# Attention's maxima through a diagonal block on the core instead of a row through DRAM, with another order of the work that fills its gaps

## Chip, core and metric

One core of a Trainium2 chip runs the whole program. The metric is the device time of one execution in microseconds (us). Engines: PE is TensorE (matrix products), DVE is VectorE, ACT is ScalarE, POOL is GpSimd, SP is the engine whose queue issues the transfers (DMA).

## What is computed

The reference is a backbone of two layers over 512 latent and 256 context tokens of width 1024: attention with a gated convolutional network behind it, then a state-space mixer with another such network. The change lies in the attention of the first layer: 16 query heads of 64 over 4 key heads, 768 tokens in all.

```python
s = jnp.einsum('bqhgd,bkhd->bhgqk', q, k).astype(jnp.float32) * (HEAD_DIM ** -0.5)
p = jax.nn.softmax(s, axis=-1).astype(v.dtype)
return jnp.einsum('bhgqk,bkhd->bqhgd', p, v)
```

Latent queries see all 768 keys, context queries the 256 context keys. The softmax needs each query's largest score, or some value near it, to be taken off before the exponential. Query and key gains are eight times the usual here, so the scores are large.

## The kernel before, in words

Heads are worked on in 8 pairs. The two heads of a pair lie on partitions 0 to 63 and 64 to 127, so each product of a pair comes as two of 64 rows that run beside each other. Tensors of the exact path are split into a high and a low part and multiplied three times.

**Maxima of a pair** (`Pair.maxima`, L588 to L617). For each tile of 128 queries the score with the high parts alone (`ps_m`, L593) goes to PSUM with queries on partitions, and a reduction on DVE (L595) takes the negated largest value per query: over the latent keys into `lat` (`ma`), over the context keys into `ctx` (`mb`). A minimum on DVE (L612) joins them into `mx`; context queries take a copy (L615). Since the scores proper have keys on partitions and queries along the free dimension, the maxima must become a row. `row` (L598 to L603) writes them to DRAM as single elements (`mrow_d<-mx`, L602) and reads them back as a row on partition 0 or 64 of `mrow` (L603), for each head, first for the four latent tiles and then for the two context tiles. All transfers are issued by SP in order.

**Scores, exponential and values of a pair** (`Pair.steps`). Seven steps: six tiles of 128 keys against the 512 latent queries, and one for the context queries. In each step six score products (L664, three for each head) and then two products of a row of ones with `mrow` (L667) add up in `ps_s`: the last ones add the negated maximum of the query to every key. ACT takes the exponential (L668, `pr`), DVE adds it to a running sum (L673, L675, L679), and one step later the value products (`ps_o`, L628) use it. At the end of a pair a product with ones (`ps_sum`, L634) and some work on ACT and DVE (L637 to L641) divide by the sum. `ps_m` and `ps_s` share two PSUM tiles.

**The order of work** around this. While pair p is in its steps, the maxima of pair p+1 are computed: each step first runs one piece of `maxima`. In the gaps `fill.run` takes pieces of other work from a list in a written order: query pairs 1 to 7 and the second pair of keys (digits and `k`), and the eight pieces of the modulation (`a`, called ada). Each call has a budget in microseconds by a rough price for each piece; a piece that yields BREAK rests for some calls (`cool`). A query pair 4 to 7 first loads its weight (`wst<-in_wq`, cast on ACT, rest on POOL), multiplies (`ps_q`), and then normalises: squares on ACT, the swap of halves for the rotary step by SP (`qsw`, L527), three operations on POOL (L528 to L530), sums of squares on PE (`ssq`, L236), transposes (`rsTq`, L253) and a product on DVE (L534). An ada piece loads four weights (`in_adaB`), multiplies (`ps_ada`), rests and transposes by products of 2 columns (`ps_adt`, L134). Before the change two calls of 0.8 us lie in each step (1.45 us for the last two pairs), one ahead of the value products and one behind them. Outside a part ordered by hand, a scheduler sets the final order of each engine's instructions.

After the last pairs the output projection begins (`ps_d`); its first operands come back from DRAM (`od<-odram`).

Of the kernel before, what the change touches and what calls it, by code (L numbers as in the profile page):

```python
# [7 lines left out]
P = 128  # L8
F32 = mybir.dt.float32
# [8 lines left out]
L = 512  # L18
C = 256
# [56 lines left out]
def _r(ap):  # L76

    return ap.bitcast(F32)
# [97 lines left out]
class Fill:  # L176
# [9 lines left out]
    def run(self, us):  # L186

        self.left = min(self.left, 0.0) + us
        self.cool = {g: n - 1 for g, n in self.cool.items() if n > 1}
        for g in list(self.q):  # L190
            while self.left > 0 and g not in self.cool:
                r = next(g, None)
                if r is None:
                    self.q.remove(g)
                    break
                if r is BREAK:
                    self.cool[g] = 5
                    self.left -= 1.0
                else:
                    self.left -= r  # L200
# [178 lines left out]
def attention(g, fill, X, late):  # L379
# [174 lines left out]
    def queries(p, qs, eng):  # L554
        if qs is None:
            w = load_w(g, I["wq"][p - 4], lo_engine="pool")
            qs = t3(g, "qs")
            for h, c0, n in ((hc, L, C), (hl, 0, L)):
                ps = Bk("ps_q")
                for k in range(KT):  # L560
                    ks = slice(k * P, (k + 1) * P)
                    mm3(g, (w[0][:, ks], w[1][:, ks]), [(ps[:, :n], h[k])], k == 0, k == KT - 1)
                    yield 3 * n / 2400
                nc.scalar.copy(qs[:, c0 : c0 + n], ps[:, :n])
            yield BREAK
        yield from normed(qs, g.qn8, eng)
        qprep[p] = t3(g, "qh", F32R), t3(g, "ql", F32R)
        split(g, qs, *qprep[p])
        yield 0

    onesr = g.const.tile([P, P], F32R, name="onesr")
    nc.scalar.copy(onesr, g.ones)
    small = lambda name, dt=F32: g.p.tile([P, 2, T // P], dt, tag="mx", bufs=6, name=name)

    class Pair:

# [5 lines left out]
        def maxima(self):  # L582


            qh, kh = qprep[self.p][0], k2[self.kv][0]
            lat, ctx, mx = small("ma"), small("mb"), small("mx", F32R)
            self.mrow = g.t3p.tile([P, T], F32R, tag="mrow", bufs=2, name=f"mrow{self.p}")

            def scores(ts, k0, n, out):
                ps = Sb("ps_m")  # L590
                for i, t in enumerate(ts):
                    for e in range(2):
                        nc.tensor.matmul(ps[:, 512 * e + n * i : 512 * e + n * i + n], qh[S64[e], t * P : (t + 1) * P],  # L593
                                         kh[S64[e], k0 : k0 + n], start=True, stop=True)
                nc.vector.reduce_max(out[:, :, ts[0] : ts[-1] + 1], ps.rearrange("p (e t k) -> p e t k", e=2, k=n),  # L595
                                     axis=AX.X, negate=True)

            def row(t0, t1):  # L598
                for e in range(2):
                    dr = g.dp.tile([1, T], F32, tag="mrow", bufs=4, name="mrow_d")  # L600
                    c = slice(t0 * P, t1 * P)
                    nc.sync.dma_start(dr[0, c].rearrange("(t p) -> p t", p=P), _r(mx[:, e, t0:t1]))  # L602
                    nc.sync.dma_start(_r(self.mrow[64 * e : 64 * e + 1, c]), dr[:, c])  # L603

            for t in (0, 2):
                scores((t,), 0, L, lat)
                yield
                scores((t + 1,), 0, L, lat)
                yield
                scores((t, t + 1), L, C, ctx)  # L610
                yield
            nc.vector.tensor_tensor(mx[:, :, :4], lat[:, :, :4], ctx[:, :, :4], ALU.min)  # L612
            row(0, 4)
            scores((4, 5), L, C, lat)
            nc.vector.tensor_copy(mx[:, :, 4:], lat[:, :, 4:])  # L615
            row(4, 6)
            yield  # L617

        def steps(self):

# [36 lines left out]
            for t in range(7):  # L657
                ps, pr = Sb("ps_s"), g.t3p.tile([P, 1024], F32, tag="pr", bufs=3, name="pr")
                for q0, n, k0, off in (((0, L, t * P, 0),) if t < 6 else ((L, C, L, 0), (L, C, L + P, C))):
# [3 lines left out]
                        for e in range(2):  # L663
                            nc.tensor.matmul(outs[e], a[S64[e], k], b[S64[e], q], start=i == 0, stop=False)  # L664
                    for e in range(2):
                        r = slice(64 * e, 64 * e + 1)
                        nc.tensor.matmul(outs[e], onesr[r], self.mrow[r, q], start=False, stop=True)  # L667
                nc.scalar.activation(pr, ps, AF.Exp)  # L668
                if t == 0:
                    po = Bk("ps_o")  # L670
# [45 lines left out]
        g.oT.append((hl_, hc_))  # L716

    adas = list(fill.q)
    fill.q = [kgen if o == "k" else adas.pop(0) if o == "a" else qgen[int(o)] for o in "12a3a4ka5a6a7aaa"]
    g.o = []  # L720
    pairs = [Pair(p) for p in range(NH // 2)]

# [8 lines left out]
    for p in range(NH // 2):  # L731
        m = iter(())
        if p < 7:
# [1 line left out]
            if p == 3:  # L735
                fill.require(kgen)
            m = pairs[p + 1].maxima()
        us = .8 if p < 6 else 1.45
        for t, todo in enumerate(pairs[p].steps()):
            next(m, None)  # L740
            fill.run(us)
            if late_step:
                late_step()
            late_step = todo
            if t == 0:
                next(m, None)
                if p == 6:
                    for i in range(5):
                        osplit(i)
                    late()  # L750
            if p == 7 and t == 3:
                osplit(5)
                osplit(6)
            fill.run(us)
# [670 lines left out]
```

## Time and profile before

| | |
|---|---|
| median of 3 runs | 2021.26 us (2016.94 to 2025.56) |
| profiled execution | 2016.52 us |
| its span, first to last instruction | 2014.7 us |
| mean granted PE clock | 0.973 |
| attention with maxima (116 to 480 us) | 364 us |
| busy: PE, DVE, ACT, POOL | 96%, 66%, 41%, 15% |

The profile is one execution. A group of instructions is named by its line, engine, operation and the tiles it writes and reads (`ps_s<-mrow,onesr`). PEld is PE's weight load, which runs beside products. The granted clock is the share of full speed that PE was given. A plain float32 product shows twice in the profile and once in the instruction order.

### The profile page before, as it was taken

How to read it: one execution, taken by the hardware profiler on the slowest of the kernel's cores; microseconds unless marked ns; L12 is line 12 of the kernel's file. 1: busy time of each engine (PE TensorE's matmuls, PEld its weight loads, DVE VectorE, ACT ScalarE, POOL GpSimd, SP SyncE). 2: the span in 40 equal slices, each digit the busy share in tenths (PEclk: the TensorE clock that was granted, in tenths of full speed). 3: DMA queues.
4: the chain of work that ended last, by engine and by line, in shares of the span. 5: the costliest groups of instructions: out<-in, count | busy, mean ns of one | idle time of the engine just before them, and what ended most of it. 6: DMA issues, size and time to landing. Idle time of an engine off the chain costs nothing.

```text
span 2014.7 us, 27655 instructions
## 1 busy us (share of the span) xinstructions
PE 1941.6 (96%) x10844; PEld 1565.3 (78%) x10844; DVE 1333.2 (66%) x1954; ACT 825.0 (41%) x1426; POOL 300.2 (15%) x272
## 2 busy tenths in 40 slices
PE   8989799999999999999998999999999999999999
PEld 6854444467888888888888888888888888888887
DVE  5545546666877777676558777877679565656565
ACT  3523323423522222222236766666667343232321
POOL 2231110101200000000003222333335130000000
PEclk8979789799999999999999999999999999999999
DMA  8252322510344443442112443334344323323332
GB/s 320 89 105 46 44 66 84 142 37 29 135 127 133 129 125 120 132 126 74 63 53 85 131 126 105 91 100 125 115 135 138 100 72 101 94 94 96 100 98 84
DMA packets 86290, 210.13 MB, mean 104 GB/s; under 512 B 21744, under 2 KB 27264, under 8 KB 86032
## 3 DMA queue, kind: packets, MB, share of 16 engines
q1 hardware_dynamic: 86160, 208.36, 34.7%
q8 instruction: 85, 1.39, 0.3%
q14 instruction: 45, 0.37, 0.1%
HBM read 198.84 MB, written 6.86 MB: 102 GB/s over the span
## 4 chain that ended last, share of the span: by engine, by line
PE 69%; DVE 12%; DMA 7%; issue 4%; POOL 2%; ACT 2%; SPq 0%; POOLq 0%; DVEq 0%; ACTq 0%
PE ps_up L105 10%; PE ps_up L106 10%; PE ps_up L108 10%; PE ps_d L105 6%; PE ps_d L106 6%; PE ps_d L108 6%; DMA mrow_d<-mx 3%; PE ps_in L108 2%; PE ps_in L105 2%; PE ps_in L106 2%; DVE xf L951 2%; PE ps_o L628 2%; PE ps_s L664 1%; DMA wst<-in_wq 1%; DVE ht L281 1%
## 5 line engine op out<-in xcount | busy, mean ns | idle before, releaser
L87 DVE TENSOR_TENSOR wl<-wst,wh 128x1024 fp32r<-128x1024 f32 x205 | 252.7, 1233 | 276.4 <-PE ps_up L106 123.2
L85 ACT CAST wh<-wst 128x1024 fp32r<-128x1024 f32 x211 | 221.0, 1048 | 456.5 <-DMA wst<-in_wup 324.8
L106 PE MATMUL ps_up<-hlf,wh 128*128 128x512 f32 x1008 | 357.3, 354 | 0.0
L105 PE MATMUL ps_up<-hhf,wh 128*128 128x512 f32 x1008 | 357.2, 355 | 0.0
L108 PE MATMUL ps_up<-hhf,wl 128*128 128x512 f32 x1008 | 356.6, 354 | 0.0
L105 PEld LDWEIGHTS ps_up<-hhf,wh 128*128 128x128 f32 x1008 | 190.8, 189 | 26.2
L106 PEld LDWEIGHTS ps_up<-hlf,wh 128*128 128x128 f32 x1008 | 190.7, 189 | 26.1
L108 PEld LDWEIGHTS ps_up<-hhf,wl 128*128 128x128 f32 x1008 | 190.5, 189 | 25.7
L105 PE MATMUL ps_in<-hhs,wh 128*128 128x512 f32 (+1 forms) x560 | 204.9, 366 | 0.6 <-ACT raw L948 0.6
L108 PE MATMUL ps_in<-hhs,wl 128*128 128x512 f32 (+1 forms) x560 | 200.1, 357 | 0.0
L106 PE MATMUL ps_in<-hls,wh 128*128 128x512 f32 (+1 forms) x560 | 199.3, 356 | 0.0
L105 PE MATMUL ps_d<-hdh,wh 128*128 128x512 f32 (+1 forms) x568 | 194.3, 344 | 1.6 <-DVE X L777 1.3
L106 PE MATMUL ps_d<-hdl,wh 128*128 128x512 f32 (+1 forms) x568 | 194.0, 342 | 0.3 <-DVE hdl L87 0.3
L108 PE MATMUL ps_d<-hdh,wl 128*128 128x512 f32 (+1 forms) x568 | 193.8, 342 | 0.0
L777 DVE SCALAR_TENSOR_TENSOR X<-ps_d,mod,X 128x512 f32<-128x512 f32 (+1 forms) x240 | 132.7, 583 | 30.6 <-PE ps_d L108 30.1
L105 PEld LDWEIGHTS ps_d<-hdh,wh 128*128 128x128 f32 x568 | 106.3, 188 | 17.1 <-DVE X L777 1.6
L106 PEld LDWEIGHTS ps_d<-hdl,wh 128*128 128x128 f32 x568 | 106.6, 188 | 16.4 <-DVE hdl L87 0.6
L105 PEld LDWEIGHTS ps_in<-hhs,wh 128*128 128x128 f32 x560 | 106.4, 190 | 15.8 <-issue 1.2
L108 PEld LDWEIGHTS ps_in<-hhs,wl 128*128 128x128 f32 x560 | 106.3, 190 | 14.9
L108 PEld LDWEIGHTS ps_d<-hdh,wl 128*128 128x128 f32 x568 | 106.6, 188 | 14.2
L167 DVE SCALAR_TENSOR_TENSOR junk<-wada,cb 128x1024 f32<-128x1024 f32 x96 | 116.6, 1214 | 1.1 <-ACT cb L159 0.8
L106 PEld LDWEIGHTS ps_in<-hls,wh 128*128 128x128 f32 x560 | 106.3, 190 | 13.7
(338 smaller groups left out, 3558.6 us busy)
## 6 DMA issues: line engine op xcount, KB each, us to landing
wst<-in_wup SPq DMA_DIRECT2D x88, 512.0 KB
wada<-in_adaT SPq DMA_DIRECT2D x48, 512.0 KB
wst<-in_win SPq DMA_DIRECT2D x48, 512.0 KB
wst<-in_wdown SPq DMA_DIRECT2D x44, 512.0 KB
wada<-in_adaB SPq DMA_DIRECT2D x32, 512.0 KB
E<-ad SPq DMA_DIRECT2D x64, 256.0 KB
ec<-ead SPq DMA_DIRECT2D x64, 128.0 KB
wst<-in_wout SPq DMA_DIRECT2D x16, 512.0 KB
```

The source lines that it names most:

```text
L85: keep(nc.scalar.copy(hi, src))
L87: keep(eng.tensor_tensor(lo, src, _r(hi), ALU.subtract))
L105: mm(out, wh, ah, start=first, stop=False)
L106: mm(out, wh, al, start=False, stop=False)
L108: mm(out, wl, ah, start=False, stop=last)
L167: g.tc.keep_in_program_order(nc.vector.scalar_tensor_tensor(junk, w, 1.0, cb[:, v * D : (v + 1) * D], ALU.mult, ALU.mult, accum_out=md[:, ...
L281: nc.vector.scalar_tensor_tensor(t[:, c0:c1], ap, g.moda[layer][ca][:, m, v : v + 1], rs[:, c0:c1], ALU.mult, ALU.mult)
L628: nc.tensor.matmul(po[S64[e], :n], v, pr[:, 512 * e + off : 512 * e + off + n], start=first, stop=last)
L664: nc.tensor.matmul(outs[e], a[S64[e], k], b[S64[e], q], start=i == 0, stop=False)
L777: nc.vector.scalar_tensor_tensor(ap, o[:, c0:c1], gate[:, m, v : v + 1], ap, ALU.mult, ALU.add)
L951: nc.vector.scalar_tensor_tensor(cv, raw[:, tap : tap + n], par(f"sw{tap}", j), cv, ALU.mult, ALU.add)
```

## The change

The row through DRAM goes. Instead DVE builds, for each pair, a tile `diag` of 128 partitions by 768: for the head on partitions 64e to 64e+63 it has twelve blocks of 64 by 64, each a diagonal with the negated maxima of 64 queries. A product of a 64-row block of ones with it (L670) adds to each key the column's only entry. For that the maxima of the two halves of a query tile are put below each other by four minima of 64 partitions (`mz`), and two products with an identity (`id2`), both operands broadcast, write `diag`. Context maxima come first instead of last.

The order changes too. One piece of maxima in each step, then the value products of the step before, then one call of `fill.run` with 1.75 us (2.9 us for the last two pairs). A resting piece rests for 3 calls instead of 5. A query pair rests once between loading its weight and multiplying. The list of the filling work has ada pieces further back.

```diff
@@ Fill.run
-                    self.cool[g] = 5
+                    self.cool[g] = 3
@@ queries
             w = load_w(g, I["wq"][p - 4], lo_engine="pool")
+            yield BREAK
@@
+    id2 = g.const.tile([P, HD], F32, name="id2")
+    for h in S64:
+        nc.scalar.copy(id2[h], g.ident[h, h])
-    small = lambda name, dt=F32: g.p.tile([P, 2, T // P], dt, tag="mx", bufs=6, name=name)
+    small = lambda name, dt=F32: g.p.tile([P, 2, T // P], dt, tag="mx", bufs=4, name=name)
@@ Pair.maxima
-            lat, ctx, mx = small("ma"), small("mb"), small("mx", F32R)
-            self.mrow = g.t3p.tile([P, T], F32R, tag="mrow", bufs=2, name=f"mrow{self.p}")
+            lat, ctx, mz = small("ma"), small("mb"), small("mz")
...
-            def row(t0, t1):
-                for e in range(2):
-                    dr = g.dp.tile([1, T], F32, tag="mrow", bufs=4, name="mrow_d")
-                    c = slice(t0 * P, t1 * P)
-                    nc.sync.dma_start(dr[0, c].rearrange("(t p) -> p t", p=P), _r(mx[:, e, t0:t1]))
-                    nc.sync.dma_start(_r(self.mrow[64 * e : 64 * e + 1, c]), dr[:, c])
-
+            scores((4, 5), L, C, lat)
+            nc.vector.tensor_copy(ctx[:, :, 4:], lat[:, :, 4:])
+            yield
             for t in (0, 2):
                 scores((t,), 0, L, lat)
                 yield
                 scores((t + 1,), 0, L, lat)
                 yield
                 scores((t, t + 1), L, C, ctx)
+                if t:
+                    for e in range(2):
+                        for h in range(2):
+                            nc.vector.tensor_tensor(mz.rearrange("p h t -> p t h")[S64[e], :, h], lat[S64[h], e],
+                                                    ctx[S64[h], e], ALU.min)
+                    self.diag = g.t3p.tile([P, T], F32R, tag="mrow", bufs=2, name=f"diag{self.p}")
+                    v = self.diag.rearrange("p (t h q) -> p t h q", h=2, q=64)
+                    for h in range(2):
+                        nc.vector.tensor_tensor(v[:, :, h], id2.unsqueeze(1).broadcast_to([P, T // P, 64]),
+                                                mz[:, h].unsqueeze(2).broadcast_to([P, T // P, 64]), ALU.mult)
                 yield
-            nc.vector.tensor_tensor(mx[:, :, :4], lat[:, :, :4], ctx[:, :, :4], ALU.min)
-            row(0, 4)
-            scores((4, 5), L, C, lat)
-            nc.vector.tensor_copy(mx[:, :, 4:], lat[:, :, 4:])
-            row(4, 6)
-            yield
@@ Pair.steps
-                        r = slice(64 * e, 64 * e + 1)
-                        nc.tensor.matmul(outs[e], onesr[r], self.mrow[r, q], start=False, stop=True)
+                        nc.tensor.matmul(outs[e], onesr[S64[e]], self.diag[S64[e], q], start=False, stop=True)
@@
-    fill.q = [... for o in "12a3a4ka5a6a7aaa"]
+    fill.q = [... for o in "123a4k5a6a7aaaaa"]
@@
-        us = .8 if p < 6 else 1.45
+        us = 1.75 if p < 6 else 2.9
         for t, todo in enumerate(pairs[p].steps()):
             next(m, None)
-            fill.run(us)
             if late_step:
                 late_step()
             late_step = todo
             if t == 0:
-                next(m, None)
```

Lines behind the change move on by 1 to 4: scores stand on L668 after (L664 before), the product with the maxima on L670 (L667), the maxima's products on L596 (L593), values on L632 (L628).

First place: PE between the last product of pair 5 (counted from 0) and the product with the maxima in the first step of pair 6. Before (`mrow_2774` is the row of pair 6; its maxima products already lie before these rows):

```order
L667 MATMUL ps_s<-mrow_2469,onesr 128x256 x2
L134 MATMUL ps_adt<-cst,ada_sb 128x2 x4
L628 MATMUL ps_o<-pr,v_728 64x512 x2
L634 MATMUL ps_sum<-acc,ones 64x512 x2
L134 MATMUL ps_adt<-cst,ada_sb 128x2 x4
L253 MATMUL rsTq<-cst,rbq 128x128 x6
L664 MATMUL ps_s<-qh,kh_2092 128x512 x2
L664 MATMUL ps_s<-qh,kl_2093 128x512 x2
L664 MATMUL ps_s<-ql,kh_2092 128x512 x2
L667 MATMUL ps_s<-mrow_2774,onesr 128x512 x2
```

After (`diag_3001` is pair 6's):

```order
L670 MATMUL ps_s<-diag_2654,onesr 128x256 x2
L596 MATMUL ps_m<-kh_1975,qh 128x256 x4
L632 MATMUL ps_o<-pr,v_728 64x512 x2
L638 MATMUL ps_sum<-acc,ones 64x512 x2
L253 MATMUL rsTq<-cst,rbq 128x128 x2
L668 MATMUL ps_s<-qh,kh_1975 128x512 x2
L668 MATMUL ps_s<-qh,kl_1976 128x512 x2
L668 MATMUL ps_s<-ql,kh_1975 128x512 x2
L632 MATMUL ps_oc<-pr,v_727 64x256
L670 MATMUL ps_s<-diag_3001,onesr 128x512 x2
```

The last maxima product of the next pair has moved into the last step; between it and the product that needs its result lie the rows shown.

Second place: DVE near the same boundary, while pair 5 is in its steps. Before, the end of pair 6's maxima (the minimum on L612, the copy on L615) with what lies between and behind:

```order
L612 TENSOR_TENSOR mx<-ma,mb 128x2x4
L87 TENSOR_TENSOR wl<-wst,wh 128x1024
L243 TENSOR_TENSOR rsu<-rsy,rsa 128x12
L244 SCALAR_TENSOR_TENSOR rsu<-rsy,rsu 128x12
L247 SCALAR_TENSOR_TENSOR rbq<-rsu,rsy 128x768
L675 TENSOR_TENSOR acc<-acc,pr 128x1024
L595 TENSOR_REDUCE ma<-ps_m 128x2x2
L145 TENSOR_TENSOR mod_90<-ps_adt,par 128x8
L615 CAST mx<-ma 128x2x2
```

After, pair 6's maxima from the last reduction on, with the two rows ahead:

```order
L87 TENSOR_TENSOR wl<-wst,wh 128x1024
L130 COPY ada_sb<-ps_ada 128x512
L598 TENSOR_REDUCE mb<-ps_m 128x2x2
L682 TENSOR_TENSOR accc<-pr 128x512
L614 TENSOR_TENSOR mz<-ma,mb 64x6 x4
L534 TENSOR_TENSOR qs<-qs,rsTq 128x256
L619 TENSOR_TENSOR diag_3001<-id_731,mz 128x6x64 x2
L643 TENSOR_TENSOR o_2684<-ps_o,y 128x512
```

The maxima now end in one go with four minima and the two products that write the diagonal, with one product of the rotary chain (L534) between.

Third place: SP's queue around the load of a query weight. Before:

```order
L602 DMA mrow_d<-mx 128x4x1 x2
L603 DMA mrow_1901<-mrow_d 1x512 x2
L602 DMA mrow_d<-mx 128x2x1 x2
L603 DMA mrow_1901<-mrow_d 1x256 x2
L122 DMA wada<-in_adaB 128x1024 x2
L654 DMA odram_993<-o_1885 128x768
L95 DMA wst<-in_wq 128x1024
L527 DMA qsw<-qs 32x512 x4
```

After:

```order
L658 DMA odram_995<-o_1572 128x768
L122 DMA wada<-in_adaB 128x1024 x2
L95 DMA wst<-in_wq 128x1024
L122 DMA wada<-in_adaB 128x1024 x3
L527 DMA qsw<-qs 32x512 x4
L122 DMA wada<-in_adaB 128x1024 x2
```

The transfers of the maxima are gone from SP's queue, and ada loads stand between the weight load and the swap.

More of the change, by code (lines that the diff above doesn't have):

```diff
@@ L718, in attention @@
     adas = list(fill.q)
-    fill.q = [kgen if o == "k" else adas.pop(0) if o == "a" else qgen[int(o)] for o in "12a3a4ka5a6a7aaa"]
+    fill.q = [kgen if o == "k" else adas.pop(0) if o == "a" else qgen[int(o)] for o in "123a4k5a6a7aaaaa"]
     g.o = []
```

## The prediction

> **What bounds the kernel now.** I read the page first, for the busy shares and the row of granted clock. The columns of its first row are busy microseconds, share and instructions; the second has one digit for each fortieth of the span, 50.4 us.
>
> ```profile
> PE 1941.6 (96%) x10844; PEld 1565.3 (78%) x10844; DVE 1333.2 (66%) x1954; ACT 825.0 (41%) x1426; POOL 300.2 (15%) x272
> PEclk8979789799999999999999999999999999999999
> ```
>
> TensorE (PE) is the bound. But from the third to the eighth digit, where attention runs, its clock is granted at 0.7 to 0.9; from about 400 us on it is whole. So the second view is the windows of attention, cut where the clock falls (columns: length; busy us of PE, PEld, DVE, ACT, POOL; clock; DMA share; GB/s).
>
> ```profile
> 116.00:480.00 364.00, 332.76 (x1729) 178.37 (x1727) 206.52 (x277) 116.32 (x159) 40.37 (x23) 0.88 0.33 74
> 120.00:144.00 24.00, 15.46 (x63) 6.24 (x62) 7.04 (x11) 4.95 (x7) 2.21 (x1) 0.57 0.84 134
> 164.00:176.00 12.00, 8.99 (x47) 5.85 (x45) 4.44 (x6) 3.58 (x7) 0.00 (x0) 0.86 0.04 2
> 205.00:232.00 27.00, 16.65 (x62) 8.84 (x62) 11.65 (x17) 6.02 (x10) 6.18 (x4) 0.56 0.48 77
> 257.00:267.00 10.00, 8.43 (x31) 4.03 (x29) 4.17 (x6) 4.02 (x7) 0.00 (x0) 0.66 0.05 2
> 276.00:287.00 11.00, 7.95 (x32) 4.41 (x31) 7.00 (x7) 3.31 (x5) 7.87 (x4) 0.69 0.39 121
> 287.00:341.00 54.00, 52.39 (x299) 27.45 (x298) 32.38 (x45) 18.56 (x25) 4.59 (x3) 1.00 0.26 72
> 341.00:348.00 7.00, 5.52 (x21) 2.49 (x21) 2.40 (x3) 1.08 (x2) 0.00 (x0) 0.76 0.03 1
> 371.00:392.00 21.00, 21.00 (x83) 12.20 (x83) 13.22 (x20) 6.09 (x7) 3.03 (x2) 0.51 0.55 51
> 392.00:396.00 4.00, 2.39 (x13) 1.10 (x11) 2.42 (x6) 2.66 (x5) 0.00 (x0) 0.99 0.91 293
> 396.00:480.00 84.00, 84.00 (x450) 51.43 (x450) 53.02 (x77) 25.61 (x35) 0.00 (x0) 1.00 0.15 47
> ```
>
> Of the 364 us of attention PE is idle for 31.2, nearly all of it in the eight stretches here that are not fully busy. On top, busy time at a lower clock is lost: busy times one minus clock gives 6.6, 1.3, 7.3, 2.9, 2.5 and 1.3 us in the six stretches that hold both idle time and a clock under 0.9, together 21.9, and 21.00 x 0.49 = 10.3 us in 371 to 392, where PE was not idle at all. Each idle microsecond thus costs 21.9 / (31.2 - 1.6 - 1.6) = 0.78 us more.
>
> Who ended the idle time: the chain that ended last (start, length, what), and the waits within attention (total, times, longest).
>
> ```profile
> 112.94 1.24 DVE mx L612
> 114.20 9.43 DMA mrow_d<-mx
> 123.64 5.12 DMA mrow<-mrow_d
> 197.45 16.73 DMA wst<-in_wq
> 270.41 6.93 DMA wst<-in_wq
> 390.92 3.86 DMA od<-odram
> PEld ps_s L667 <- DMA mrow<-mrow_d: 22.2, 10, 9.4
> PE ps_m L593 <- ACT pr L668: 6.8, 1, 6.8
> ACT wh L85 <- DMA wst<-in_wq: 24.9, 2, 15.5
> ```
>
> The round trip of the maxima through DRAM takes 14.5 us for the first pair, and the product on L667 waits for it. The other cause is a query weight load: ScalarE sits before its cast for 24.9 us in two waits, the exponentials stand behind that cast, and PE waits for them. That load took 16.7 us where the maxima's transfers of single elements ran beside it, and 6.9 us later.
>
> **The change, part by part.** *The DRAM trip goes.* Its 8 pairs x 2 heads x 4 = 64 transfers, and their waits, leave SP's queue. What is next ahead of step 0's exponential is a chain on VectorE, costed below. I take all idle stretches as gone but 392 to 396, where the od loads for the output projection are awaited, which the change leaves: 31.2 - 1.6 = 29.6 us. The part of this that hangs on the weight loads (the last 8 us of idle in 205 to 232, and 276 to 287) could stay; then 8 + 3 idle and 7 + 2.5 of clock come back, 20 us. I take it as gone, because the load is issued without the maxima's transfers in front and beside it.
>
> *The clock behind the idle stretches* comes back with them: 21.9 us. The 10.3 us of 371 to 392 I leave in: there PE had work, but much of it in products of 2 columns, and that work stays.
>
> ```profile
> 371.37 1.68 PE L134 MATMUL ps_adt<-cst,ada_sb 128*128 128x2 f32 x8
> ```
>
> [...]
>
> *The product with the maxima* is of 1 row by 128 before and of 64 by 128 after. Its price is read from the starts in the timeline, a full-clock step and a place where a score product is followed by a maxima product directly (start, length, what).
>
> ```profile
> 180.62 0.50 PE L664 MATMUL ps_s<-qh,kh 64*128 64x512 f32 x2
> 180.96 0.40 PE L664 MATMUL ps_s<-qh,kl 64*128 64x512 f32 x2
> 181.19 0.39 PE L664 MATMUL ps_s<-ql,kh 64*128 64x512 f32 x2
> 181.51 0.49 PE L667 MATMUL ps_s<-mrow,onesr 1*128 1x512 f32 x2
> 181.94 0.50 PE L593 MATMUL ps_m<-kh,qh 64*128 64x512 f32 x2
> 182.37 0.50 PE L105 MATMUL ps_q<-hha,wh 128*128 128x512 f32 x1
> 117.24 0.40 PE L664 MATMUL ps_s<-ql,kh 64*128 64x512 f32 x2
> 117.47 0.39 PE L593 MATMUL ps_m<-kh,qh 64*128 64x512 f32 x2
> ```
>
> Between two products of 64 rows it is 0.23 us (180.96 to 181.19, and 117.24 to 117.47 across the lines). Into the 1-row product it is 0.32, out of it 0.43. With 64 rows throughout both should be 0.23: 0.09 + 0.20 = 0.29 us less for each group. There are 8 pairs x (6 + 2) = 64 groups, 18.6 us at most. Not every one is followed by a 64-row product (the last pair has no maxima behind it), and at the lower bound the 1-row form costs nothing extra, so 0 to 18.6; I take 14, near the row at full clock.
>
> [...]
>
> *VectorE's new work.* Per pair one minimum becomes four on 64 partitions, and two products of 384 elements come in.
>
> ```profile
> L612 DVE TENSOR_TENSOR mx<-ma,mb x8: 156/160/1226, 112.9 to 422.9; 128x8 fp32r<-128x8 f32 x8
> L534 DVE TENSOR_TENSOR qs<-qs,rsTq x8: 414/550/689, 237.7 to 386.7; 128x512 f32<-128x512 f32 x4, 128x256 f32<-128x256 f32 x4
> L595 DVE TENSOR_REDUCE ma<-ps_m x40: 1209/1225/1227, 96.0 to 425.0; 128x2 f32<-128x1024 f32 x32, 128x4 f32<-128x1024 f32 x8
> L679 DVE TENSOR_TENSOR accc<-pr x8: 681/689/2017, 163.5 to 475.5; 128x512 f32<-128x512 f32 x8
> ```
>
> 256 elements take 0.41 us and 512 take 0.69, so 384 with broadcast operands about 0.55. Four minima at 0.16, two products at 0.55, less one minimum: 1.58 us a pair, 12.6 in all. VectorE is busy for 206.5 of 364 us; 219 of about 300 still leaves it under PE. On the path lies only the end of the maxima. Behind a pair's last maxima product come a reduction, the sum of two halves, four minima and the two products: 1.22 + 0.69 + 4 x 0.2 (start to start) + 2 x 0.55 = 3.8 us. Meanwhile PE has the value products, the sums, some filling work and six score products.
>
> ```profile
> 202.41 1.08 PE L628 MATMUL ps_o<-pr,v 128*64 128x512 f32 x4
> 203.31 1.03 PE L634 MATMUL ps_sum<-acc,ones 128*64 128x512 f32 x4
> 204.27 1.50 PE L236 MATMUL ssq<-cst,qsq 128*128 128x2 f32 x12
> ```
>
> These are 0.90 and 0.96 us, and six score products 0.89 (180.62 to 181.51). At the boundary with least filling (pair 5 to 6, two transposes, about 0.3) the cover is 3.1 us, 0.7 short, and 1.1 with the 0.41 us product that stands between there. Then L670 waits at the head of PE's queue, behind it stand all of PE's products in order, and the first exponential of the pair waits on ScalarE. Elsewhere filling of 1 to 3 us covers it. Eight times 0.5: +4 us, between 0 and the third rival's 21.
>
> *The order of the filling work*, one call of 1.75 us instead of two of 0.8, a pause of 3 calls instead of 5, maxima and values back to back: the same products in sum, so 0, with rivals four and five as its price. The buffers (6 to 4) and the set-up of id2 and its two copies: nothing, they lie beside the value products ahead of the first pair.
>
> *Sum*, against the profiled execution's 2016.5 us (span 2014.7): -29.6 - 21.9 - 14 + 4 = -61.5, so 1955.0 us. The median of the runs, 2021.3, lies 4.7 us (0.2%) above that execution; I carry over about half of that: 1957 us.
>
> **The rivals.** *One: the clock falls only behind idle time*, as in six of the seven slow stretches; then 371 to 392 recovers as well, 1957 - 10.3 = 1947 us. Against it stands that stretch itself. *Two: the 64-row product is no cheaper than the 1-row one* (the kinds of neighbours and not its rows make the gaps): 1957 + 14 = 1971 us. *Three: the diagonal is late.* If at each boundary VectorE also has a sum of 1.22 us and a product of 0.69 (rows above) queued ahead, the chain is 5.7 us against 3.1: 2.6 x 8 = 21 us idle in place of 4, and at 0.78 us of clock for each, 1957 + 17 + 0.78 x 21 = 1990 us. For it: VectorE's share rises to 73%. Against: most boundaries have more filling. *Four: filling in one lump holds longer runs of 2-column products, and the clock stays low without idle time*, as from 371: all 21.9 us stay, 1979 us.
>
> *Five, slower: the rotary chain reaches the head of VectorE's queue.* The product on L534 waits for GpSimd, which waits for the swap of halves on SP.
>
> ```profile
> 218.15 2.42 SPq L527 DMA_DIRECT2D qsw<-qs  x4
> 226.35 1.33 POOL L530 TENSOR_TENSOR qs<-qs,qsw 128x512 f32<-128x512 f32 x1
> ```
>
> From 218.15 to 227.68 that is 9.5 us. The pause now covers three steps of about 1.46 + 1.0 + 1.75 = 4.2 us, 12.6 in all. If the ada loads that stand ahead of the swap on SP wait for their buffers, the pause is eaten up; VectorE then holds back maxima and sums. With the whole chain bare eight times (seven query pairs, one of keys) 76 us come on top: 1957 + 76 = 2033 us. It decides from 9.3 us of each chain on; nothing in the waits of before comes near that. That the trip through DRAM is not removed is no case: no such transfer is left in the order of SP's queue.
>
> **How the numbers follow.** Forecast 0.46, one 0.18, two 0.12, three 0.08, four 0.12, five 0.04. The range goes from rival one with the full 18.6 us of products, no late diagonal and a little of the od wait gone (1947 - 4.6 - 4 - 2.4 = 1936) up to rival three, 1990. Left out are five and the tails. A measurement of this kernel can tell about 0.5%, 10.1 us, from no change. All cases but five are faster by more than that, less 0.01 for a tail: 0.95; five gives 0.03 slower and 0.01 within, so 0.02 within.
>
> **What would show it.** In the profile after: attention shorter by about 60 us, no stretch with idle time over 2 us at a pair's start, the clock row at 9 in most of the third to eighth slices, L670 starting 0.23 us after the score product before it. I am wrong if idle time in attention stays above 15 us, if the low clock stays without idle time, or if the end of attention moves by less than 25 us.

## The result and the profile after

The median is 1951.74 us (1945.84 to 1956.94, 4 runs), against 2023.41 us of the kernel before (2016.94 to 2027.59, 4 runs): a ratio of 0.9648, 95% interval 0.9607 to 0.9688. The profiled execution took 1954.1 us with a span of 1952.0 us and a mean granted clock of 0.987; so the span is 62.7 us shorter than the 2014.7 us of before. The prediction had 61.5 us less, against the same execution.

The page of the profile after: PE's busy time fell by 51 us, DVE's rose by 11, and the row of granted clock has no digit under 8.

```profile
PE 1890.7 (97%) x10844; PEld 1555.9 (80%) x10844; DVE 1343.8 (69%) x1994; ACT 825.4 (42%) x1428; POOL 295.6 (15%) x272
PEclk8989999999999999999999999999999999999999
```

The windows of attention after, cut where the clock falls (columns as before: length; busy us of PE, PEld, DVE, ACT, POOL; clock; DMA share; GB/s). The last row is the whole.

```profile
126.00:131.00 5.00, 1.89 (x16) 1.10 (x15) 4.20 (x5) 0.50 (x2) 3.01 (x2) 1.00 0.62 205
131.00:143.00 12.00, 12.00 (x58) 7.01 (x58) 8.47 (x13) 6.93 (x11) 4.61 (x3) 0.57 0.28 80
143.00:192.00 49.00, 48.87 (x330) 30.45 (x328) 38.88 (x51) 20.27 (x26) 13.23 (x9) 1.00 0.21 70
192.00:197.00 5.00, 4.86 (x22) 3.10 (x23) 4.38 (x12) 2.06 (x5) 0.00 (x0) 0.66 0.00 0
197.00:324.00 127.00, 124.97 (x813) 68.10 (x811) 94.98 (x136) 51.28 (x70) 17.51 (x10) 1.00 0.40 138
126.30:413.20 286.90, 280.32 (x1724) 165.59 (x1723) 217.26 (x316) 115.01 (x159) 38.06 (x23) 0.98 0.28 95
```

Of 286.9 us PE is idle for 286.90 - 280.32 = 6.6, and two stretches have a low clock: 12.00 x 0.43 + 4.86 x 0.34 = 6.8 us lost. Before it was 31.2 and about 34 us.

But attention also begins later. The next rows are the first score product of the tile's group and the last of `ps_oc`, of before and then of after (columns: duration min/median/max, first and last start).

```profile
L664 PE MATMUL ps_s<-qh,kh x128: 381/496/793, 116.7 to 473.3; 64*128 64x512 f32 x96, 64*128 64x256 f32 x32
L628 PE MATMUL ps_oc<-pr,v x64: 379/634/690, 172.3 to 479.2; 128*64 128x256 f32 x64
```
```profile
L668 PE MATMUL ps_s<-qh,kh x128: 275/494/792, 126.3 to 407.4; 64*128 64x512 f32 x96, 64*128 64x256 f32 x32
L632 PE MATMUL ps_oc<-pr,v x64: 379/379/687, 163.7 to 412.2; 128*64 128x256 f32 x64
```

From first to last start, attention went from 479.2 - 116.7 = 362.5 to 412.2 - 126.3 = 285.9 us: 76.6 us less. It begins 9.6 us later, and from its last start to the end of the span it is 1539.8 us in place of 1535.5. In sum -76.6 + 9.6 + 4.3 = -62.7. The last of these is within what the kernels below show there, all with the same work (1531.3 to 1544.4). The 9.6 are not noise. ScalarE's first rows in the timeline of before, with the first projection product on PE:

```profile
2.03 0.30 ACT L572 CAST onesr<-ones 128x128 fp32r<-128x128 f32 x1
4.49 0.63 ACT L435 ACTIVATE acc<-X 128x512 f32<-128x512 f32 x1 [2.16 <-DMA X<-in_xT]
18.49 0.80 PE L105 MATMUL ps_l<-hha,wsh 128*128 128x512 f32 x1 [0.19 <-ACT hha L290]
```

and after:

```profile
13.90 0.50 ACT L576 COPY id<-cst 64x64 f32<-64x64 f32 x2 [11.58 <-DMA cst<-in_cst]
14.41 0.63 ACT L435 ACTIVATE acc<-X 128x512 f32<-128x512 f32 x1
28.49 0.49 PE L105 MATMUL ps_l<-hha,wsh 128*128 128x512 f32 x1 [1.05 <-ACT hha L290]
```

The two copies that set up `id2` need the identity from `cst`, for whose transfer ScalarE waits 11.58 us. The scheduler put them ahead of the squares of X on ScalarE; those waited behind them for 9.9 us, and the first product starts 10.0 us later. In the order of ScalarE the place could be read ahead of any run:

```order
L573 CAST onesr<-ones 128x128
L576 COPY id_731<-cst 64x64 x2
L435 ACTIVATE acc<-X 128x512
```

### The profile page after: what moved, and what is told of

Read it like the earlier page. It is cut to its first block, busy times and chain, and to the rows that moved or that the text cites. A ratio compares the mean times of both kernels' runs of the same rounds, so it can differ in the third digit from the quotient of the medians.

```text
span 1952.0 us, 27591 instructions
## 1 busy us (share of the span) xinstructions
PE 1890.7 (97%) x10844; PEld 1555.9 (80%) x10844; DVE 1343.8 (69%) x1994; ACT 825.4 (42%) x1428; POOL 295.6 (15%) x272
## 4 chain that ended last, share of the span: by engine, by line
PE 66%; DVE 15%; issue 6%; POOL 3%; DMA 3%; ACT 2%; SPq 1%; POOLq 0%; DVEq 0%; ACTq 0%
PE ps_up L105 10%; PE ps_up L106 10%; PE ps_up L108 10%; PE ps_d L105 6%; PE ps_d L108 6%; PE ps_d L106 6%; DVE xf L952 2%; PE ps_s L668 2%; PE ps_o L632 2%; DVE E L1061 1%; DVE Bf L952 1%; DMA E<-ad 1%; DVE wl L87 1%; DVE ht L281 1%; PE ps_wo L105 1%
```

## The experiments

One table of all. Ratios are to the kernel before on the same chip. From one profiled execution each: the start of the first projection product, attention from its first score product to its last start of `ps_oc`, and in attention PE's idle time and what the clock took (busy time times one minus the clock, added up in windows of 2 us).

| kernel | median us | ratio, 95% interval | first product | attention | idle | clock |
|---|---|---|---|---|---|---|
| before | 2023.4 | 1 | 18.5 | 362.5 | 31.2 | 34.5 |
| after | 1951.7 | 0.9648, 0.9607 to 0.9688 | 28.5 | 285.9 | 6.6 | 6.8 |
| e1 diagonal only | 1951.0 | 0.9653, 0.9624 to 0.9681 | 29.6 | 284.1 | 5.8 | 0.0 |
| e2 filling only | 2032.8 | 1.0056, 1.0024 to 1.0088 | 18.6 | 369.6 | 44.3 | 28.0 |
| e3 one row | 1979.6 | 0.9796, 0.9761 to 0.9831 | 28.3 | 313.1 | 4.7 | 14.8 |
| e4 33 rows | 1949.4 | 0.9658, 0.9622 to 0.9695 | 28.5 | 287.2 | 6.1 | 8.1 |
| e5 diagonal twice | 1960.5 | 0.9684, 0.9667 to 0.9700 | 28.7 | 291.1 | 11.6 | 7.2 |
| e6 every fourth | 1953.4 | 0.9651, 0.9632 to 0.9670 | 28.4 | 281.7 | 5.0 | 3.4 |
| e7 2 columns | 2015.4 | 0.9958, 0.9925 to 0.9990 | 28.9 | 354.6 | 7.3 | 41.9 |
| e8 wide | 1974.1 | 0.9751, 0.9729 to 0.9772 | 29.0 | 306.2 | 7.1 | 8.2 |
| e9 1 row, run | 1982.4 | 0.9778, 0.9740 to 0.9816 | 28.6 | 319.2 | 7.8 | 20.5 |
| e10 every fifth | 1943.9 | 0.9588, 0.9566 to 0.9611 | 28.6 | 279.5 | 4.5 | 1.7 |
| e11 trip unawaited | 1976.9 | 0.9752, 0.9722 to 0.9782 | 28.6 | 311.3 | 27.7 | 7.9 |
| e12 two fills | 1962.5 | 0.9676, 0.9649 to 0.9704 | 28.8 | 296.0 | 10.4 | 11.8 |

**Which half of the change does it.** The first kernel takes the diagonal and leaves all of the filling as it was; the second the other way round.

```diff
 e1 (against after)
-                    self.cool[g] = 3
+                    self.cool[g] = 5
-    ... "123a4k5a6a7aaaaa"
+    ... "12a3a4ka5a6a7aaa"
-        us = 1.75 if p < 6 else 2.9
+        us = .8 if p < 6 else 1.45
             next(m, None)
+            fill.run(us)
...
+                next(m, None)
 (no yield BREAK behind load_w; context maxima last, minima and diagonal behind them)
```

> Before with the diagonal product alone: filling work, its pauses, its list and the order of the maxima as before (two steps of the maxima at a pair's first step, context maxima last). Theory (the trip through DRAM is what made the idle time and the low clock, and the 1-row product the slow starts): about the time of after, 1945 to 1962 us, and no idle stretch over 2 us at a pair's start. Rival (the new order of the filling work is what freed the weight loads): their 20 us of idle time and low clock stay, 1965 to 1985 us, with waits for wst of 15 to 25 us on ScalarE. Rival (the low clock without idle time comes from the filling in small portions): a low stretch of some 10 us near 370 less the saved time, 1960 to 1965 us.

```diff
 e2 (against before)
-                    self.cool[g] = 5
+                    self.cool[g] = 3
             w = load_w(g, I["wq"][p - 4], lo_engine="pool")
+            yield BREAK
-    ... "12a3a4ka5a6a7aaa"
+    ... "123a4k5a6a7aaaaa"
-        us = .8 if p < 6 else 1.45
+        us = 1.75 if p < 6 else 2.9
             next(m, None)
-            fill.run(us)
```

> Before with the filling work of after alone (one call of 1.75 us, pause of 3, the pause behind the weight load, the new list); the maxima still go through DRAM and the product is of 1 row. Theory: the trip stays, so idle time of 20 us or more in attention, 2000 to 2030 us. Rival (the order of the filling is what brings the gain): 1960 to 1985 us.

The diagonal alone gives the whole gain: 0.9653 against 0.9648. The new filling alone is 0.6% slower than before, with 44.3 us of idle time. Its waits in attention (total us, times, longest):

```profile
PEld ps_s L668 <- DMA mrow<-mrow_d: 28.8, 11, 9.4
PE ps_s L668 <- DMA mrow<-mrow_d: 24.8, 9, 9.4
```

Its 2032.8 us lie just above the 2030 that its theory allowed, and far from the rival's 1960 to 1985. So the gain comes from the diagonal, which replaces the trip through DRAM and the product of 1 row at once (the next two experiments take these apart), and the order of the filling work is worth nothing by itself beside it. In e1 the wait of ScalarE for query weights is 9.8 us in 4, none over 5.5, against 24.9 of before: most of that wait went without the pause and the new list (in after it is 1.6).

**Wait or traffic.** What the trip cost could be the waiting for it or what its transfers do to others. This kernel is after with the transfers of before put back, where nobody uses what they bring.

```diff
+                    dx = g.dp.tile([2, T], F32, tag="mrowx", bufs=2, name="mrow_x")
+                    for t0, t1 in ((0, 4), (4, 6)):
+                        for e in range(2):
+                            dr = g.dp.tile([1, T], F32, tag="mrow", bufs=4, name="mrow_d")
+                            c = slice(t0 * P, t1 * P)
+                            nc.sync.dma_start(dr[0, c].rearrange("(t p) -> p t", p=P), lat[:, e, t0:t1])
+                            nc.sync.dma_start(dx[e : e + 1, c], dr[:, c])
                     self.diag = ...
```

> After with the trip of before added again as traffic alone: per pair the same transfers of single elements to DRAM and their copies (ending in DRAM), which nobody waits for; the product takes the diagonal. If the transfers by themselves slow the query weight loads and what stands behind them on SP's queue: 10 to 25 us slower than after, 1962 to 1977 us, with waits for wst on ScalarE of 15 us or more. If only the wait for the trip costs: within 4 us of after, 1948 to 1956 us.

1976.9 us, 25 us over after, and 25.4 us more attention, nearly all of it idle time (27.7 against 6.6). The transfers of e11 (packed size, median us from issue to landing), and PE's longest waits in its attention, and, in the last row, what SP's queue waits for ahead of the copies (L622):

```profile
wst<-in_wq SPq DMA_DIRECT2D x3, 512.0 KB, 6.0
mrow_d<-ma SPq DMA_DIRECT2D x16, 2.0 KB, 11.4
mrow_d<-ma SPq DMA_DIRECT2D x16, 1.0 KB, 11.5
```
```profile
PE ps_m L596 <- ACT qh L85: 9.4, 1, 9.4
PE ssq L236 <- ACT qsq L523: 5.0, 1, 5.0
PE ps_ada L128 <- DMA wada<-in_adaB: 4.9, 4, 2.3
SPq L622 <- DMA mrow_d<-ma: 57.7, 13, 9.8
```

A transfer of 512 single elements takes 11.4 us, and its copy behind it holds SP's queue until it has landed, 57.7 us in 13 waits, so weights, ada loads and the swaps come late; one query weight took 13.39 us on the chain that ended last (4.6 is the median of after). ScalarE's waits for weights were only part of what was expected: 7.9 us for `in_wq` and 10.9 for `in_w_o`, where I had put 15 on the first alone. A small part is a wait all the same: VectorE sat 6.6 us in four waits until the transfers had read the small tiles that it writes next. By this a third of the 76.6 us can come from the traffic alone, without the product's wait for the row. It is an estimate: the transfers of e11 are issued at another moment than those of before, all at the end of a pair's maxima.

**One row against 64.** Two kernels change how many rows of `diag` and of the ones the product on L670 uses, and both scale the exponent by the same 0.1.

```diff
-  nc.tensor.matmul(outs[e], onesr[S64[e]], self.diag[S64[e], q], ...)
+  r = slice(64 * e, 64 * e + 1)          # e4: 64 * e + 33
+  nc.tensor.matmul(outs[e], onesr[r], self.diag[r, q], ...)
-  nc.scalar.activation(pr, ps, AF.Exp)
+  nc.scalar.activation(pr, ps, AF.Exp, scale=.1)
```

> After with a product of only the first row of each half (1 row by 128 in place of 64 by 128) and the exponent scaled by 0.1 so that it stays finite: of the maxima only one query in 64 is subtracted. Order, waits and VectorE's work are those of after. Theory (a product of 1 row between products of 64 rows costs 0.3 to 0.4 us of starts per group, some 60 groups): 18 to 26 us slower than after, 1970 to 1978 us. Rival (rows cost nothing, the neighbours made the gaps): within 4 us of after, 1948 to 1956 us.

> After with a product of the first 33 rows of each half, exponent scaled by 0.1 to stay finite: of the maxima 33 queries in 64 are subtracted. If the extra time of the 1-row product is a change of the array's row setting that 33 rows share with 64: the time of after, 1948 to 1956 us. If it goes by the number of rows: half of the 1-row form's extra, 1960 to 1966 us. If any product whose rows differ from its neighbours' pays: 1970 to 1978 us.

One row is 0.9796 - 0.9648 = 1.5% or 30 us slower than after, more than the forecast 18 to 26, and 28 us slower than 33 rows on the same chip (0.9796 - 0.9658, of 2025 us); 33 rows are as fast as 64 (0.9658 and 0.9648). From 33 to 64 the rows cost nothing here, then, but 1 and 33 are not the same: the product's median length is 0.39 us with 64 rows, 0.40 with 33 and 0.50 with one (128 of each). In full-clock steps, of after and then of e3 (start, length, what):

```profile
166.73 0.40 PE L668 MATMUL ps_s<-ql,kh 64*128 64x512 f32 x2
166.96 0.39 PE L670 MATMUL ps_s<-diag,onesr 64*128 64x512 f32 x2
167.19 0.39 PE L596 MATMUL ps_m<-kh,qh 64*128 64x512 f32 x2
167.51 0.65 PE L632 MATMUL ps_o<-pr,v 128*64 128x512 f32 x2
```
```profile
168.50 0.40 PE L668 MATMUL ps_s<-ql,kh 64*128 64x512 f32 x2
168.82 0.50 PE L671 MATMUL ps_s<-diag,onesr 1*128 1x512 f32 x2
169.26 0.50 PE L596 MATMUL ps_m<-kh,qh 64*128 64x256 f32 x4
169.69 1.08 PE L632 MATMUL ps_oc<-pr,v 128*64 128x256 f32 x8
```

The three starts behind the last score product come after 0.23, 0.23 and 0.32 us with 64 rows, and after 0.32, 0.44 and 0.43 with one: 0.41 us for each group, and 64 groups make 26 us at most. In attention e3 is 27.2 us longer than after: 8.0 of them are clock, 1.9 less are idle, and the 21 that are left fit such starts. The lower clock is there in each of four executions: 0.979 to 0.984 over the whole span, against 0.984 to 0.989 for after and 0.984 to 0.988 for 33 rows. By the times of the pair of runs 33 rows behave like 64, and one row does not. What the expectations here and below call a change of the row setting stands in the traces as these wider starts (0.32 to 0.44 us beside a 1-row product or where 128 rows follow 64, against 0.23 between products of 64) and as nothing else; that a setting of the array changes there is not shown.

**What lowers the clock.** Rival one said: only idle time. Three kernels put extra products into five places of attention where PE is busy.

```diff
             fill.run(us)
+            if t == 3 and 0 < p < 6:
+                px = Bk("ps_x")
 e7
+                for i in range(32):
+                    nc.tensor.matmul(px[:, 2 * i : 2 * i + 2], g.ones, g.ones[:, :2], start=True, stop=True)
 e8
+                for i in range(17):
+                    nc.tensor.matmul(px[:, :512], onesr, hl[i % KT][0][:, :512], start=True, stop=True)
 e9
+                    nc.tensor.matmul(px[:, :512], onesr[:1], hl[i % KT][0][:1, :512], start=True, stop=True)
```

> After with 32 extra products of 128 by 128 by 2 columns (4.0 us of TensorE) in five places, the fourth step of pairs 1 to 5, into a bank that nobody reads. Theory (a run of products of 2 columns makes the clock fall although TensorE is never idle): 20 us of their own and some 10 us at half clock behind each, 5 x 5 = 25 us: 1990 to 2005 us. Rival one of the prediction (the clock falls only behind idle time): their own 20 us, 1970 to 1976 us, clock 1.00 behind each.

> After with 17 extra products of 128 by 128 by 512 columns (3.9 us of TensorE) in the same five places. Both theories: their own 20 us, 1970 to 1976 us, and a clock of 1.00 behind each; a low clock behind these would say that it is the pause of the other engines and not the shape.

> After with 17 extra products of 1 row by 128 columns by 512 (3.9 us of TensorE) in the five places of the two runs before, into a bank that nobody reads. Theory (the clock follows how much of the array works, so a product of 1 row counts nearly as idle, and the maxima product of before helped to bring the clock down): a stretch of 6 to 16 us at half clock behind each, 1995 to 2020 us, as with 2 columns. Rival (only narrow outputs and idle time bring it down, rows don't count): their own 20 us and the changes of the row setting, 1972 to 1980 us, clock 1.00 behind each.

The first of the five places in each, cut where the run of extra products is 4 us old (e7, e8, e9):

```profile
181.16:185.16 4.00, 4.00 (x38) 4.00 (x36) 0.65 (x1) 2.37 (x3) 2.80 (x1) 1.00 0.50 145
185.16:195.66 10.50, 10.50 (x45) 7.94 (x45) 2.04 (x2) 1.02 (x1) 3.77 (x3) 0.51 0.23 72
```
```profile
180.73:184.68 3.95, 3.95 (x18) 3.00 (x16) 0.66 (x1) 2.38 (x3) 2.85 (x1) 1.00 0.44 138
184.68:194.68 10.00, 10.00 (x78) 6.68 (x79) 6.51 (x6) 2.77 (x3) 4.67 (x3) 1.00 0.26 79
```
```profile
179.73:183.73 4.00, 4.00 (x18) 3.03 (x17) 0.56 (x1) 2.37 (x3) 2.81 (x1) 1.00 0.52 145
183.73:187.73 4.00, 4.00 (x15) 1.69 (x14) 1.45 (x2) 1.02 (x1) 0.09 (x1) 0.57 0.57 184
```

In all of these rows PE is busy without a gap. The five places, one by one (start of the extra run; the fall of the clock, in us behind it; how long the clock is at 0.50):

| place | e7, 2 columns | e8, wide | e9, 1 row |
|---|---|---|---|
| pair 1 | 181.16; 4.0; 10.2 | 180.73; no fall | 179.73; 4.3; 3.4 |
| pair 2 | 223.53; 2.6; 13.7 | 215.16; no fall | 215.98; 2.2; 6.8 |
| pair 3 | 268.18; 2.3; 13.7 | 250.22; no fall | 254.42; 4.7; 3.4 |
| pair 4 | 312.74; 2.1; 13.7 | 285.20; no fall | 291.19; 2.0; 6.8 |
| pair 5 | 366.63; 2.9; 20.5 | 329.08; no fall for 9.7 us | 338.42; 2.6; 6.8 |

The wide products leave the clock at 1.00 for over 5 us behind them in all five places; behind the fifth it falls at 338.8, 3.3 us after the start of sixteen transposes of 2 columns that are the kernel's own. Behind 2 columns and behind one row it falls in all five, 2.0 to 4.7 us after the run's start. In e7 and e9 the first three places are clean; at the fourth and fifth, 2-column products of the kernel's own stand less than 1 us ahead of the run. Thus idle time is not all that brings the clock down: it falls to 0.50 behind products of 2 columns or of one row as well, in ten places of ten. That it goes by how much of the array works, as the theory of e9 has it, is not shown by this. The sizes were off. In e7 each plain float32 product is two in the profile, so a run held 64 products and took 10 to 12 us and not 4; the kernel lost 41.9 us to the clock (after 6.8). In e9 the low stretches were only 3.4 to 6.8 us long, and its 1982 us lie between the two forecasts; by times alone e9 and e8 can't be told apart, by the clock they can (20.5 us lost against 8.2).

The lengths show something more. The second place of e9, and the fifth of e8 where the clock falls:

```profile
214.73:218.14 3.41, 3.41 (x15) 2.51 (x14) 1.12 (x1) 1.99 (x3) 0.00 (x0) 1.00 0.35 96
218.14:224.97 6.83, 6.83 (x21) 4.06 (x21) 0.71 (x1) 1.41 (x2) 0.00 (x0) 0.50 0.27 107
224.97:228.38 3.41, 3.41 (x28) 1.30 (x26) 2.34 (x3) 0.00 (x0) 0.00 (x0) 1.00 0.18 44
```
```profile
335.39:338.80 3.41, 3.41 (x30) 2.78 (x29) 2.96 (x6) 1.12 (x3) 0.00 (x0) 1.00 0.02 5
338.80:342.21 3.41, 3.41 (x14) 1.13 (x16) 2.79 (x4) 1.78 (x2) 0.00 (x0) 0.50 0.52 154
```

In the fourteen traces the clock is low in 60 stretches between 90 us and the end of attention. Each lasts 1 to 7 times 3.41 us, and within one execution their starts lie whole multiples of 3.413 us apart (in before 122.42, 170.21 and 207.76: 14 and 11 of them). So within an execution the clock changed only at steps of 3.413 us, and how many narrow products fall into one step depends on where it begins. A stretch of one step more or less, 1.7 us lost (half of 3.41), in a single execution says little about a kernel.

**Is the diagonal late?** VectorE writes the two products of each pair twice.

```diff
-                    for h in range(2):
+                    for h in (0, 1, 0, 1):
                         nc.vector.tensor_tensor(v[:, :, h], id2..., mz..., ALU.mult)
```

> After with the two diagonal products of each pair written twice: 1.1 us more on VectorE between the last reduction of a pair's maxima and its first maxima product. Theory (filling, values and score products cover the chain at every boundary but the first, where the wait of 3.1 us was bare): 1 to 6 us slower than after, 1952 to 1958 us. Rival three of the prediction (the chain is bare, or nearly so, at each boundary): 8 x 1.1 x 1.78 = 16 us slower, 1965 to 1972 us, with waits of the maxima product for the diagonal at most pairs.

1960.5 us; attention is 5.2 us longer, 5.0 of them idle. The times put it 7 us over after (0.9684 - 0.9648), a little more than the theory had (1 to 6) and half of rival three's 16. PE's wait for the diagonal, in e5:

```profile
PE ps_s L670 <- DVE diag L619: 8.7, 5, 5.7
```

Of 8.7 us in five waits 5.7 are one wait, at the first pair; the others share 3.0. So in after, where the two other waits take 0.5 us, all boundaries but the first have cover.

**The first boundary.** After has its longest wait there (PE, DVE and POOL in the timeline of after; the second and third row are two of the four minima of the first):

```profile
125.30 3.92 DVE L614 TENSOR_TENSOR mz<-ma,mb 64x6 f32<-64x6 f32 x4
125.48 2.32 DVE L614 TENSOR_TENSOR mz<-ma,mb 64x6 f32<-64x6 f32 x1
127.82 1.21 DVE L614 TENSOR_TENSOR mz<-ma,mb 64x6 f32<-64x6 f32 x1
125.41 2.38 POOL L87 TENSOR_TENSOR wl<-wst,wh 128x1024 fp32r<-128x1024 f32 x1
127.75 1.26 POOL L530 TENSOR_TENSOR raw<-raw,qsw 128x512 f32<-128x512 f32 x1
126.83 0.40 PE L668 MATMUL ps_s<-ql,kh 64*128 64x512 f32 x2
129.25 1.03 DVE L619 TENSOR_TENSOR diag<-id,mz 128x384 fp32r<-128x384 f32 x2
130.33 0.50 PE L670 MATMUL ps_s<-diag,onesr 64*128 64x512 f32 x2 [3.11 <-DVE diag L619]
```

Four minima whose median is 0.16 us each took 3.92 here, and a low clock (0.57 over 12 us) lies behind the 3.11 us of idle time. The two slow minima begin 0.07 us after an operation of GpSimd and end 0.01 to 0.02 us after it. Of the other pairs in after only the one at 190.66 has GpSimd beside its minima: there the four take 1.76 us, at the others 0.69. Over the kernels with the diagonal it is the same: at the first pair the four take 1.70 to 4.44 us in the ten traces where GpSimd runs beside them, and 0.70 in the two where it doesn't (e6 and e10, below). That VectorE waited for GpSimd there is my reading of these times; a kernel that moves only GpSimd's work was not run. Two kernels let the first pair's maxima start earlier among the value projection's pieces.

```diff
     for i, _ in enumerate(vals):
-        if i % 6 == 5:
+        if i % 4 == 3:          # e10: i % 5 == 4
             next(m, None)
```

> After with the maxima of the first pair a step at every fourth piece of the value projection in place of every sixth, so that they end earlier. Theory (the first boundary costs 3.1 us of idle time and, behind it, 12 us at 0.57 of the clock, 5 us): 6 to 9 us faster than after, 1942 to 1948 us, no wait for the diagonal at the first pair and no low clock near 131. Rival (the low clock there comes from products of 2 columns at the boundary and not from the wait): 3 us faster, 1948 to 1950 us, with the low clock still there.

> After with the maxima of the first pair a step at every fifth piece of the value projection (every sixth in after, every fourth in the run before). Theory (at every fourth the maxima products stood so close that TensorE waited for the reductions; at every fifth neither wait is bare): 3 to 8 us faster than after, 1944 to 1949 us. Rival (the wait only moves, as at every fourth): within 2 us of after, 1950 to 1954 us.

At every fourth piece nothing is won: 0.9651. The wait at the diagonal is gone (0.5 us is left of it), but PE idles for 2.5 us in three waits for the maxima's reductions between 108 and 112.4, the clock is low for 3.4 us from 112.2, and attention begins 3.8 us later for the 4.2 that it is shorter. At every fifth piece it is 0.9588, against 0.9648 of after; the two intervals overlap slightly (0.9611 and 0.9607), so faster is likely and not settled. The trace shows 5.0 us of it: attention is 6.4 us shorter and begins 1.4 us later.

```profile
128.26 0.40 PE L668 MATMUL ps_s<-ql,kh 64*128 64x512 f32 x2
128.49 0.40 PE L670 MATMUL ps_s<-diag,onesr 64*128 64x512 f32 x2
```

In e10 the product with the maxima follows 0.23 us behind the score product at the first pair too. It has the lowest median of this study, about 4.1% under before.

**Lumps of filling.** Rival four blamed them for a low clock. This kernel has two calls in each step again.

```diff
-                    self.cool[g] = 3
+                    self.cool[g] = 5
-        us = 1.75 if p < 6 else 2.9
+        us = .8 if p < 6 else 1.45
             next(m, None)
+            fill.run(us)
```

> After with the filling in two calls of 0.8 us a step (1.45 in the last pairs) and a pause of 5 calls, as before; maxima order, list and the pause behind the weight load as in after. If lumps of filling are what lowers the clock (rival four): 5 to 8 us faster, 1944 to 1947 us, no low clock. If filling in small pieces costs as much in changes of the row setting as it saves in clock: within 3 us of after, 1949 to 1955 us.

Neither forecast: 1962.5 us, with more idle time (10.4 us) and more lost to the clock (11.8), where e1, also with two calls, loses nothing to it. Its interval (0.9649 to 0.9704) overlaps that of after, so slower is not settled; of the gain of 5 to 8 us that rival four needed nothing is seen, in the time or in the trace. Of its loss, 6.8 us lie behind the first boundary (5.2 in after). Why e12 idles and loses more than e1, which also has the old list, the old order of the maxima and no pause behind the weight load, is open.

## Why the prediction was right, point by point

The sign and the cause hold: e1 shows that the diagonal alone brings the gain, e2 that the trip kept means the idle time kept. The sum, -61.5, lies 1.2 us from the measured -62.7 of the spans, but that closeness is luck: attention gained 76.6, 15 more than the sum, and the later start (9.6) and the time behind attention (4.3, within its spread) took nearly all of that back. The 76.6 are 24.6 of idle time, 27.7 of clock and 24.3 that are left for PE's work. One of the signs named ahead failed: the first pair's start has an idle stretch of 3.1 us, over the 2 us allowed.

- *The DRAM trip goes*, -29.6: measured -24.6 (31.2 to 6.6). The 20 us that hung on the weight loads went, as taken; e11 shows that the traffic alone brings 25 us back, most of it as idle time.
- *The clock behind the idle stretches*, -21.9: measured about -28 (34.5 to 6.8), since the 10.3 us of 371 to 392, which I left in, went as well, and 5.2 are still lost behind the first boundary. I had named the 2-column products there, and e7 shows the clock at 0.50 for 10.2 to 20.5 us behind runs of such products. What I did not see is that the 1-row products between them can bring it down too: in e9 it is at 0.50 for 3.4 to 6.8 us behind runs of them. Whether they made this stretch is likely and not shown: e1, with the filling of before and 64-row products, has none, and e3 falls (from 330.8) where after, with the same sums of squares and the same transposes of 2 columns in the same order, stays at full clock (307.7 to 317). But the steps of the clock cut these products at other points in the two, and in e8 the clock is at 0.50 for 3.4 us behind a step that holds 1.9 us of such transposes with 64-row products around them.
- *The product with the maxima*, -14 with 18.6 at most: the step that was mis-sized. By the sum above 24.3 are left for it, and e3 has 21 us more in starts than after, and is 28 to 30 us slower than e4 and after. The bound failed in two ways: it counted two gaps, and the product behind L596 pays too (0.43 against 0.32); and it did not count the clock, which takes 8.0 us more in e3 than in after.
- *VectorE's new work*, +12.6: measured +11.5 (205.8 to 217.3 in attention). The wait, +4 as eight times 0.5: it is one wait of 3.1 us at the first pair, with 5.2 us of clock behind it, and next to nothing elsewhere (3.6 us in three waits in all). The chain was priced with minima of 0.2 us; beside GpSimd they took up to 2.3.
- *The order of the filling work*, 0: right beside the diagonal (e1 equals after).
- *The set-up of id2 and its two copies*, "nothing, they lie beside the value products ahead of the first pair": this step failed. They stand third on ScalarE's queue and wait for `cst`; the start is 10.0 us late. All twelve kernels with the copies show it and the two without them (before and e2) do not: 28.3 us and more against 18.5 and 18.6, e1 and e2 on one chip among them. No kernel was run that only moves the copies, so what it would bring back in the end is not measured.

Rival one's time (1947) is as near as the forecast's, but its rule is refuted by e7 and e9 (ten falls in ten places with PE busy). Rival two falls with e3, rival three with e5, rival four with the 6.8 us that after itself loses to the clock, and with e12. Rival five was not seen: in after ScalarE waits for the rotary product on L534, 2.9 us in two waits, and VectorE has no wait for GpSimd ahead of it.

## What to carry to other kernels

A product of one row between products of 64 cost twice here: in wider starts on both sides (0.41 us for each group), and in clock (8.0 us more lost in e3 than in after); behind runs of such products, or of products of 2 columns, the clock fell to 0.50 in ten places of ten. Padding it to the rows of its neighbours can be faster although it does more arithmetic (after is 30 us faster than e3). Tiny transfers cost beyond their own wait (25 us in e11), since whatever stands behind them in their queue comes late (a query weight took 13.39 us, against a median of 4.6 in after). And a set-up instruction has the price of the place the scheduler gives it (10.0 us at the start here): read the head of every queue for what each entry waits for, however small the entry is.

## What the runs showed that I had not expected

- The clock fell in ten of ten runs of narrow or 1-row products on a busy PE, 2.0 to 4.7 us after their start, to 0.5, and in none of the five runs of wide ones.
- In the fourteen traces it fell and rose on a grid of 3.41 us (60 stretches, each 1 to 7 times that long).
- A kernel with 33 rows in the product with the maxima takes the time of one with 64 (0.9658 and 0.9648); a single row costs 0.41 us a group more.
- At the first pair, one of four minima on VectorE took 2.3 us where the median is 0.16, and ended 0.01 us behind the operation of GpSimd that ran beside it.
